# Feed-forward accumulators: the two column halves of a projection go to two PSUM banks instead of one

## The chip, the cores and the metric

The program runs on one core of a Trainium2 chip. Inside the core, TensorE (PE in the profile) multiplies matrices and writes the sums into PSUM, eight banks of 128 partitions by 512 fp32 columns; ScalarE (ACT) and VectorE (DVE) read PSUM and work in SBUF; the SyncE queue (SP) issues the transfers from memory. Engines run side by side and wait for one another by semaphores. The metric is the time of one execution in microseconds (us), lower being better.

## The reference, cut to what matters

The model is a two-layer encoder trunk over 256 tokens of width 1024, in float32. Each layer is a SwiGLU feed-forward, a token-mixing part and a second feed-forward, all added to the residual stream `h` after a gate; so there are four feed-forwards. The part that the change concerns:

```python
def swiglu(u, wg, wu, wd):
    return (jax.nn.silu(u @ wg) * (u @ wu)) @ wd
...
for l in range(DEPTH):                       # DEPTH = 2
    u = modulate(rmsnorm(h, norm_ffn1[l]), ...)
    h = h + 0.5 * (1.0 + mod[:, :, 2]) * swiglu(u, ffn1_wg[l], ffn1_wu[l], ffn1_wd[l])
    ...                                      # token mixing, ends in  mixed @ w_out[l]
    u = modulate(rmsnorm(h, norm_ffn2[l]), ...)
    h = h + 0.5 * (1.0 + mod[:, :, 8]) * swiglu(u, ffn2_wg[l], ffn2_wu[l], ffn2_wd[l])
```

`wg` and `wu` are 1024 x 2816, `wd` is 2816 x 1024.

## The kernel before

**Three matmuls for one.** Every fp32 weight and activation is split into a rounded high part and a remainder (`hi` and `lo` for weights, `uh` and `ul` for the normalised input `u`), and a product is the sum of hi x uh, hi x ul and lo x uh. `mm3` issues these three matmuls, each of 128 x 128 weights against 256 token columns, into the same 128 x 256 region of PSUM. This is the block of three that the title of the change speaks of.

**One feed-forward.** `ffn` runs over `j`, the 11 column groups of 256 of `wg` and `wu`. For one `j`, `proj` computes the gate projection: eight contraction chunks `k`, in each two column halves `f`, each a block of three, thus 48 matmuls. They go into one PSUM bank named `pg`: half `f = 0` in columns 0 to 255, half `f = 1` in columns 256 to 511. ACT applies silu to the whole bank (into `sg`); then 48 matmuls compute the up projection into another bank, `pu`; DVE multiplies `sg` by `pu`; `gated` splits the product into high and low parts (`g`). Then TensorE takes down projections (`out_unit`, tile `dn`) of earlier `j`, whose `g` has long been ready: 48 matmuls each, in 16 blocks of three, for eight row groups `d` of the output, two `d` to a bank in four banks. The four banks of `pg` and `pu` come from a ring (`bank`) of four, those of `dn` from the other four (`acc`). The j = 1 groups of the last three feed-forwards are done as a pair (`proj2`: gate and up interleaved). The first column groups of a feed-forward are done ahead of the loop (`start`: three in the first feed-forward, `lead`: one in the others, tiles `ld`). So in the first feed-forward the loop has eight `j`, in each of the others ten, one of them the pair: 38 in all, of which 35 are not pairs.

**The last down projection** goes through the row groups in pairs: twelve matmuls for `d` = 0 and 1, then DVE adds them to `h` (line 539), then the next pair. The output projection of token mixing (tile `wo`) uses the same function.

**The order of work** is written out by hand: each engine executes its instructions in the order in which the code names them. The weights come as a stream of 1 MB transfers (`raw_w`, and `raw_a` for the modulation weights) into four buffers. `half(n, hf)` asks for half of weight unit `n`; before it returns, `need` makes sure that the splits of all halves up to seven ahead (`AHEAD`) have been issued: `hi` on ACT (line 322) and `lo` on DVE (line 323). These splits therefore stand in ACT's queue among the silus: ahead of the silu of one `j` stand the splits of weights that are needed several units later, and each waits for its transfer. Eight `hi` and eight `lo` buffers hold the split halves, and the uses of TensorE free them.

Of the kernel before, what the change touches and what calls it, by code (L numbers as in the profile page):

```python
# [10 lines left out]
ALU = mybir.AluOpType  # L11
PSUM = bass.MemoryType.PSUM

P = 128
# [68 lines left out]
def downs(j, g0):  # L83
    done = 0
    for i in range(g0, j + 1):
        lo = done
        done = i if i - lo <= 2 else lo + 2
    return range(lo, done)
# [74 lines left out]
class Trunk:  # L163
# [352 lines left out]

    def out_unit(self, accs, n, mov, first, last, gate):
        nc = self.nc
        dst = lambda d: accs[d // 2][:, (d % 2) * 256:(d % 2) * 256 + 256]

        def block(w, d, f):
            st = first and f == 0 and d % 2 == 0
            self.mm3(dst(d), [w[0][:, d * P:(d + 1) * P], w[1][:, d * P:(d + 1) * P]], mov[f], st)

        if not last:
            for f in range(2):
                w = self.half(n, f)
                for d in range(8):
                    block(w, d, f)
                    if d % 2:  # L530
                        self.tick()
            return
        ws = [self.half(n, 0, 7), self.half(n, 1, 6)]
        for b in range(4):
            for d in (2 * b, 2 * b + 1):
                for f in range(2):
                    block(ws[f], d, f)
            for d in (2 * b, 2 * b + 1):
                nc.vector.scalar_tensor_tensor(out=self.h[:, d], in0=dst(d), scalar=gate[:, d:d + 1], in1=self.h[:, d],
                                               op0=ALU.mult, op1=ALU.add)  # L540
            if self.hg is None and b == 2:
                nc.scalar.preload_act_table_set(SET_SQRT)
            self.norm_a(b)
            if b == 2 or self.hg and b:
                self.norm_b(b - 1)
        if self.hg:
            self.norm_b(3)
# [10 lines left out]
    def proj_k(self, bank, w, k, flip, banks):  # L558
        w = [t[:, k % 4] for t in w]
        for f in range(2):  # L560
            if flip:
                self.mm3(banks[f], w, [t[:, f * P:(f + 1) * P] for t in self.u(k)], k == 0, True)
            else:
                cs = slice(f * P, (f + 1) * P)
                self.mm3(bank[:, f * 256:(f + 1) * 256], [t[:, cs] for t in w], self.u(k), k == 0 and f == 0)
# [17 lines left out]
    def ffn(self, w0, gate_col, prep, start=None):  # L583
        nc = self.nc
        self.open_acc(False)
        n = w0 + 2
        pend = []

        def gated(sg):
            g = self.tk4("g", FR)  # L590
            gh, gl = (g[:, 2 * i:2 * i + 2] for i in range(2))
            flat = lambda t: t.rearrange("p a b -> p (a b)")
            self.split(flat(gh), flat(gl), sg)
            pend.append([(gh[:, f], gl[:, f]) for f in range(2)])

        def ends(f, t, b):
            v = sg[:, (f % 2) * 256:(f % 2) * 256 + 256]
            if f < 2:
                self.silu(out=v, in_=t, bias=b)
            else:  # L600
                nc.vector.scalar_tensor_tensor(out=v, in0=t, scalar=b, in1=v, op0=ALU.add, op1=ALU.mult)

        g0 = 1
        if start:
            g0 = GS
            banks = start()
            n = w0 + 2 * GS
            self.need(n, 0, 2)
            for j in range(GS):
                sg = self.tk2("sg")  # L610
                self.silu(out=sg, in_=banks[2 * j])
                nc.vector.tensor_tensor(out=sg, in0=sg, in1=banks[2 * j + 1], op=ALU.mult)
                gated(sg)
        else:
            sg = self.tk2("sg")
            self.lead(w0, ends)
            gated(sg)
        accs = None
        for j in range(g0, NJ):
            pg, pu = self.bank("pg"), self.bank("pu")  # L620
            pair = j == 1
            if pair:
                self.proj2(n, (pg, False, None), (pu, False, None))
            else:
                self.proj(pg, n)
            sg = self.tk2("sg")
            self.silu(out=sg, in_=pg)
            if not pair:
                self.proj(pu, n + 1)
            nc.vector.tensor_tensor(out=sg, in0=sg, in1=pu, op=ALU.mult)  # L630
            gated(sg)
            if j == g0:
                accs = [self.acc("dn") for _ in range(4)]
            n += 2
            for i in downs(j, g0):
                self.out_unit(accs, n, pend.pop(0), i == 0, False, None)
                n += 1
            if start and j == 7:
                nc.sync.dma_start(out=self.consts, in_=self.io["consts"])
                nc.sync.dma_start(out=self.wdt, in_=self.io["wdt"])  # L640
        gate = self.gate(gate_col, True)
        prep()
        self.out_unit(accs, n, pend.pop(0), False, True, gate)
        self.close_acc()
# [469 lines left out]
```

## Time and profile before

| | us |
|---|---|
| median of 3 runs | 1152.15 (1152.0 to 1152.48) |
| the profiled execution: its time | 1152.72 |
| its span, first to last instruction | 1151.0 |
| PE busy | 1116.2 (97%) |
| DVE busy | 893.1 (78%) |
| ACT busy | 618.0 (54%) |
| hardware DMA queue, share of 16 engines | 64.6% |

The profile is of one execution on the one core. Busy time of PE is the union of the matmuls' records; a matmul's record is about 280 ns long and overlaps the next ones, so the pace is read from the distances of the starts, or from the chain that ended last, where 48 matmuls of one tile stand as one row with their time. The granted clock is the share of TensorE's full clock that was let through. A row of a timeline reads: start in us, duration in us, engine, line, operation, output tile <- input tiles, shape, count, and in brackets how long the engine had been idle before and what released it.

### The profile page before, as it was taken

To read this page: it belongs to the slowest core of one execution; us is meant where nothing else is said; L and a number is where in the kernel's file an instruction comes from. 1 tells how busy PE (TensorE), PEld (TensorE's weight loads), DVE (VectorE), ACT (ScalarE), POOL (GpSimd) and SP (SyncE) were. 2 spreads that over 40 slices of the span, in tenths; PEclk is the share of its full clock that TensorE was granted. 3 is DMA by queue.
4 is the path that set the end of the run, shared out by engine and by line. 5 is a ranking of instruction groups with operands and counts; after the bars stand their busy time and mean duration, and the time that the engine had idled before them with its cause. 6 is when DMAs were issued, how large, how long until landed. Compare 5 with 4: busy or idle time off the path is not lost.

```text
span 1151.0 us, 22045 instructions
## 1 busy us (share of the span) xinstructions
PE 1116.2 (97%) x9316; PEld 1105.1 (96%) x9316; DVE 893.1 (78%) x1300; ACT 618.0 (54%) x870; POOL 0.2 (0%) x4
## 2 busy tenths in 40 slices
PE   1999999999999999999999999999999999999996
PEld 1999999999999999999999999999999999999996
DVE  6988896788778789888588788667886877987544
ACT  4463444586874464444466444457687546544442
POOL 0000000000000000000000000000000000000000
PEclk9999999999999999999999999999999999999999
DMA  9879898357553449999636988653754452987610
GB/s 379 342 267 369 328 374 323 126 212 286 181 186 146 184 147 375 359 347 341 225 111 262 347 325 315 252 183 139 265 200 181 168 204 77 351 330 283 238 57 37
DMA packets 39556, 282.63 MB, mean 246 GB/s; under 512 B 4385, under 2 KB 4641, under 8 KB 5409
## 3 DMA queue, kind: packets, MB, share of 16 engines
q1 hardware_dynamic: 39456, 281.22, 64.6%
q8 instruction: 73, 1.20, 0.4%
q14 instruction: 27, 0.21, 0.1%
HBM read 280.15 MB, written 1.05 MB: 244 GB/s over the span
## 4 chain that ended last, share of the span: by engine, by line
PE 96%; DVE 2%; ACT 1%; DMA 1%; issue 0%; SPq 0%; ACTq 0%; DVEq 0%
PE dn L206 21%; PE pu L206 19%; PE pg L206 19%; PE pj L206 14%; PE ld L206 8%; PE wo L206 6%; PE pv L206 4%; DVE raw_a L282 1%; PE seg L206 1%; PE nps L206 1%; PE tail L206 1%; PE sz L206 1%; DMA h<-in_x 1%; PE rn L206 1%; PE yb L206 1%; PE rs L206 0%
## 5 line engine op out<-in xcount | busy, mean ns | idle before, releaser
L323 DVE TENSOR_TENSOR lo<-raw_w,hi 128x1024 fp32r<-128x1024 f32 x368 | 441.4, 1223 | 143.4 <-ACT hi L322 143.2
L322 ACT ACTIVATE hi<-raw_w 128x1024 fp32r<-128x1024 f32 x368 | 379.7, 1053 | 240.8 <-DMA raw_w<-in_w 107.5
L206 PE MATMUL dn<-g,hi 128*128 128x256 f32 x1408 | 250.4, 279 | 0.0
L206 PEld LDWEIGHTS dn<-g,hi 128*128 128x128 f32 x1408 | 215.1, 187 | 0.0
L282 DVE CUSTOM_DVE_ANT_0 raw_a<-raw_a,cond,params 128x1024 f32<-128x1024 f32 x160 | 198.9, 1280 | 0.5 <-DMA raw_a<-in_ada 0.5
L206 PE MATMUL dn<-g,lo 128*128 128x256 f32 x704 | 196.9, 280 | 0.0
L206 PE MATMUL pg<-uh,lo 128*128 128x256 f32 x608 | 170.1, 280 | 0.0
L206 PE MATMUL pu<-uh,lo 128*128 128x256 f32 x608 | 170.1, 280 | 0.0
L206 PE MATMUL pg<-uh,hi 128*128 128x256 f32 x608 | 169.8, 279 | 0.0
L206 PE MATMUL pu<-uh,hi 128*128 128x256 f32 x608 | 169.8, 279 | 0.0
L206 PE MATMUL pg<-ul,hi 128*128 128x256 f32 x608 | 169.6, 279 | 0.0
L206 PE MATMUL pu<-ul,hi 128*128 128x256 f32 x608 | 169.6, 279 | 0.0
L206 PEld LDWEIGHTS dn<-g,lo 128*128 128x128 f32 x704 | 132.2, 188 | 0.0
L206 PE MATMUL pj<-uh,hi 128*128 128x256 f32 x448 | 126.3, 282 | 0.0
L206 PE MATMUL pj<-ul,hi 128*128 128x256 f32 x448 | 124.4, 278 | 0.0
L206 PE MATMUL pj<-uh,lo 128*128 128x256 f32 x448 | 124.4, 278 | 0.0
L206 PEld LDWEIGHTS pg<-uh,lo 128*128 128x128 f32 x608 | 114.2, 188 | 0.0
L206 PEld LDWEIGHTS pu<-uh,lo 128*128 128x128 f32 x608 | 114.2, 188 | 0.0
L206 PEld LDWEIGHTS pu<-ul,hi 128*128 128x128 f32 x608 | 114.1, 188 | 0.0
L206 PEld LDWEIGHTS pg<-ul,hi 128*128 128x128 f32 x608 | 114.1, 188 | 0.0
L206 PEld LDWEIGHTS pg<-uh,hi 128*128 128x128 f32 x608 | 113.8, 187 | 0.0
L206 PEld LDWEIGHTS pu<-uh,hi 128*128 128x128 f32 x608 | 113.8, 187 | 0.0
(189 smaller groups left out, 1788.3 us busy)
## 6 DMA issues: line engine op xcount, KB each, us to landing
raw_w<-in_w SPq DMA_DIRECT2D x184, 1024.0 KB, 5.3
raw_a<-in_ada SPq DMA_DIRECT2D x80, 1024.0 KB, 6.4
consts<-in_consts SPq DMA_DIRECT2D x1, 1216.0 KB, 7.8
h<-in_x SPq DMA_DIRECT2D x1, 1024.0 KB, 6.6
out<-fin SPq DMA_DIRECT2D x4, 256.0 KB, 2.3
cond<-in_c SPq DMA_DIRECT2D x1, 512.0 KB, 4.3
mats<-in_mats SPq DMA_DIRECT2D x1, 256.0 KB, 6.8
params<-in_params SPq DMA_DIRECT2D x1, 176.0 KB, 4.6
```

The lines of the kernel that those rows point to most:

```text
L206: self.nc.tensor.matmul(out, lhsT=lhsT, rhs=rhs, start=start, stop=True, skip_group_check=True)
L282: nc.vector.tensor_tensor_reduce(out=raw[:, f * 1024:(f + 1) * 1024], in0=raw[:, f * 1024:(f + 1) * 1024], in1=self.cond, scale=1.0, scala ...
L322: self.nc.scalar.activation(out=hi, in_=src, func=AF.Copy)
L323: self.nc.vector.tensor_tensor(out=lo, in0=src, in1=hi.bitcast(F32), op=ALU.subtract)
```

## The change

Gate and up projection of one `j` now share two banks, both named `pgu`: in each bank, columns 0 to 255 are a half of the gate projection and columns 256 to 511 the same half of the up projection. Half `f` of either goes to bank `f`, so that consecutive blocks of three alternate between the two banks. The silu and the multiplication are each done as two instructions of 256 columns, one per bank, instead of one of 512. In `out_unit` row group `d` goes to bank `d % 4` instead of `d // 2`, so that there too consecutive row groups are in different banks. No matmul, no transfer and no byte of SBUF is added, removed or moved; the paddings that place the weights at 0 and the activations at 64 modulo 256 are as they were.

```diff
@@ out_unit
-        dst = lambda d: accs[d // 2][:, (d % 2) * 256:(d % 2) * 256 + 256]
+        dst = lambda d: accs[d % 4][:, (d // 4) * 256:(d // 4) * 256 + 256]
 
         def block(w, d, f):
-            st = first and f == 0 and d % 2 == 0
+            st = first and f == 0 and d < 4
             self.mm3(dst(d), [w[0][:, d * P:(d + 1) * P], w[1][:, d * P:(d + 1) * P]], mov[f], st)
@@ proj_k
+            elif flip is None:
+                cs = slice(f * P, (f + 1) * P)
+                self.mm3(bank[f], [t[:, cs] for t in w], self.u(k), k == 0 and banks)
             else:
                 cs = slice(f * P, (f + 1) * P)
                 self.mm3(bank[:, f * 256:(f + 1) * 256], [t[:, cs] for t in w], self.u(k), k == 0 and f == 0)
@@ ffn
         for j in range(g0, NJ):
-            pg, pu = self.bank("pg"), self.bank("pu")
+            two = [self.bank("pgu") for _ in range(2)]
+            pg, pu = ([t[:, o:o + 256] for t in two] for o in (0, 256))
             pair = j == 1
             if pair:
-                self.proj2(n, (pg, False, None), (pu, False, None))
+                self.proj2(n, (pg, None, True), (pu, None, False))
             else:
-                self.proj(pg, n)
+                self.proj(pg, n, None, True)
             sg = self.tk2("sg")
-            self.silu(out=sg, in_=pg)
+            for f in range(2):
+                self.silu(out=sg[:, f * 256:(f + 1) * 256], in_=pg[f])
             if not pair:
-                self.proj(pu, n + 1)
-            nc.vector.tensor_tensor(out=sg, in0=sg, in1=pu, op=ALU.mult)
+                self.proj(pu, n + 1, None, False)
+            for f in range(2):
+                v = sg[:, f * 256:(f + 1) * 256]
+                nc.vector.tensor_tensor(out=v, in0=v, in1=pu[f], op=ALU.mult)
             gated(sg)
```

Three places in the order of the instructions matter. The first is on PE, in the first feed-forward at `j = 4`, where the gate projection ends and the up projection begins. Names carry buffer numbers here (`hi10_1_706` is the high part of the second half of weight unit 10; `pg_895` and `pu_896` are one bank each). Before, the first matmul of `pu` waits for ACT's split of its weights, which is `hi11_0_735`:

```order
L206 MATMUL pg_895<-uh_92,lo10_1_706 128x256
L206 MATMUL pu_896<-uh_92,hi11_0_735 128x256 [waits Activation_49]
L206 MATMUL pu_896<-ul_93,hi11_0_735 128x256
L206 MATMUL pu_896<-uh_92,lo11_0_736 128x256 [waits DVE_49]
L206 MATMUL pu_896<-uh_92,hi11_0_735 128x256
```

The same place in the changed kernel:

```order
L206 MATMUL pgu_898<-uh_92,lo10_1_707 128x256
L206 MATMUL pgu_897<-uh_92,hi11_0_736 128x256 [waits Activation_49]
L206 MATMUL pgu_897<-ul_93,hi11_0_736 128x256
L206 MATMUL pgu_897<-uh_92,lo11_0_737 128x256 [waits DVE_49]
L206 MATMUL pgu_898<-uh_92,hi11_0_736 128x256 [waits Activation_49]
```

The count that the first matmul of the up projection waits for is now that of the silu of bank 897 (later in ACT's order than the split), and the first block into bank 898 has a wait of its own, for the silu of bank 898; before, `pu` was another bank than the one that the silu reads.

The second place is ACT's queue around that silu. Before:

```order
L322 ACTIVATE hi13_1_897<-raw_w13_502 128x1024 [waits PE_49,Activation_49]
L322 ACTIVATE hi14_0_931<-raw_w14_629 128x1024 [waits DMAHW5_49,PE_49,Activation_49]
L203 ACTIVATE sg_959<-pg_895 128x512 [waits PE_49]
L322 ACTIVATE hi14_1_961<-raw_w14_629 128x1024 [waits Activation_49]
L322 ACTIVATE hi15_0_995<-raw_w15_649 128x1024 [waits DMAHW7_49,PE_49,Activation_49]
```

In the changed kernel:

```order
L322 ACTIVATE hi13_1_899<-raw_w13_502 128x1024 [waits PE_49,Activation_49]
L322 ACTIVATE hi14_0_933<-raw_w14_629 128x1024 [waits DMAHW5_49,PE_49,Activation_49]
L203 ACTIVATE sg_961<-pgu_897 128x256 [waits PE_49]
L203 ACTIVATE sg_961<-pgu_898 128x256 [waits PE_49]
L322 ACTIVATE hi14_1_964<-raw_w14_629 128x1024 [waits Activation_49]
```

The silu stands where it stood, now in two, behind the split of weight unit 14, which waits for that unit's transfer (`DMAHW`).

The third place is on PE in the last down projection of the first feed-forward, where row group 4 begins. Before (bank 769 is the third of four, and nothing has read it yet):

```order
L206 MATMUL dn_768<-g_2228,hi32_1_2109 128x256 x2
L206 MATMUL dn_768<-g_2228,lo32_1_2110 128x256
L206 MATMUL dn_769<-g_2228,hi32_0_2079 128x256 x2
L206 MATMUL dn_769<-g_2228,lo32_0_2080 128x256
L206 MATMUL dn_769<-g_2228,hi32_1_2109 128x256 x2
```

In the changed kernel (here bank 769 is the first of four, which also holds row group 0):

```order
L206 MATMUL dn_772<-g_2244,hi32_1_2123 128x256 x2
L206 MATMUL dn_772<-g_2244,lo32_1_2124 128x256
L206 MATMUL dn_769<-g_2244,hi32_0_2093 128x256 [waits DVE_49]
L206 MATMUL dn_769<-g_2244,hi32_0_2093 128x256
L206 MATMUL dn_769<-g_2244,lo32_0_2094 128x256
```

Row group 4 now waits for DVE's update of `h` from row group 0, which reads the same bank; row groups 5, 6 and 7 wait likewise for those from 1, 2 and 3.

## The prediction

> **What bounds the kernel now.** I read the page first, then the chain that ended last, then the list of waits, then the timeline at the ends of the gate projections. The page's busy times and the chain's shares:
>
> ```profile
> PE 1116.2 (97%) x9316; PEld 1105.1 (96%) x9316; DVE 893.1 (78%) x1300; ACT 618.0 (54%) x870; POOL 0.2 (0%) x4
> PE 96%; DVE 2%; ACT 1%; DMA 1%; issue 0%; SPq 0%; ACTq 0%; DVEq 0%
> ```
>
> TensorE is the path, so the question is at what pace it goes and where it would begin to wait. Seven pieces of the chain in order of time (start, us, tile, matmuls):
>
> ```profile
> 143.46 5.65 PE pg L206 x48
> 149.11 5.65 PE pu L206 x48
> 154.76 5.65 PE dn L206 x48
> 241.57 29.93 PE pj L206 x264
> 276.95 4.24 PE pv L206 x36
> 282.90 6.88 PE pv L206 x60
> 329.87 7.11 PE pj L206 x60
> ```
>
> In the feed-forward every piece of 48 takes 5.65 us, 117.7 ns a matmul, and no piece waits for another. `pg` and `pu` stay in one bank for 48 matmuls and `dn` changes banks every six, at the same pace. In token mixing `pj`, in one bank and with the same two operand tensors as `pg`, runs 264 matmuls at 113.4 ns; `pv`, which alternates between two banks every three matmuls, runs 36 at 117.8 ns. So there are two paces, and neither bank layout owns one of them.
>
> **Alternating the banks by itself: nothing.** By `pv` at 117.8 ns against `pg` at 117.7 the alternation costs 0.1 ns or less. It concerns 38 x 96 + 44 x 48 = 5760 matmuls, so if it moved all of them to `pj`'s pace it would save 5760 x 4.4 ns = 25 us. I take 0 and keep 25 us for the range; the second stretch of `pv` (114.7 ns, with a break in it) says that alternating banks can be found at the faster pace too.
>
> **The new wait at the up projection.** Its first block now writes a bank that the silu must have read. These rows show the normal case, the last block of half 0, the last matmul of half 1, the first of `pu`, and the silu:
>
> ```profile
> 148.47 0.28 PE L206 MATMUL pg<-uh,lo 128*128 128x256 f32 x1
> 148.83 0.28 PE L206 MATMUL pg<-uh,lo 128*128 128x256 f32 x1
> 148.95 0.28 PE L206 MATMUL pu<-uh,hi 128*128 128x256 f32 x1
> 149.15 0.60 ACT L203 ACTIVATE sg<-pg 128x512 f32<-128x512 f32 x1 [0.86 <-PE pg L206]
> L457 ACT ACTIVATE rs<-nps 128x256 f32<-128x256 f32 x6 | 2.3, 386 | 6.9 <-PE nps L206 6.9
> L203 ACT ACTIVATE sg<-pg 128x512 f32<-128x512 f32 x38 | 22.5, 592 | 40.9 <-PE pg L206 40.9
> ACT sg L203 <- PE pg L206: 40.9, 24, 4.7
> ```
>
> ACT starts 0.04 us after the matmul that it waits for has ended (148.83 + 0.28 to 149.15). A silu of 256 PSUM columns is not in the trace; the ACT copy of 128x256 out of PSUM takes 0.39, and I take that. Half 0 ends at 148.75, its silu runs from 148.79 to 149.18, and with another 0.04 PE may go at 149.22 instead of 148.95: 0.27 us. A restart costs a little more, as the only long wait of PE on ACT shows, at half the clock (the second start comes 0.39 after the first, where 0.21 is the pace):
>
> ```profile
> 27.02 0.58 PE L206 MATMUL ld<-uh,hi 128*128 128x256 f32 x1 [10.35 <-ACT hi L322]
> 27.41 0.41 PE L206 MATMUL ld<-ul,hi 128*128 128x256 f32 x1
> 28.66 0.41 PE L206 MATMUL ld<-uh,hi 128*128 128x256 f32 x1
> 32.93 0.29 PE L206 MATMUL ld<-uh,lo 128*128 128x256 f32 x1
> ```
>
> That is 0.18 us, half of it at full clock: 0.36 us per wait. The second silu ends about 149.53, when the second block (149.22 + 0.09 + 0.35 = 149.66) has not yet come, so that wait is free. Low end 0.2 us (no latency), high end 0.5 (the second wait shows too).
>
> Behind the waiting matmul stands all of TensorE's work, so the whole wait lengthens the path. Of the 38 silus three belong to pairs, which have no such wait; 35 remain. In 24 of these ACT stood ready and waited for PE, as the last row shows; in the other 11 ACT came late, which before cost nothing, because nothing but the multiplication after `pu` needed the silu.
>
> **Where ACT is late.** The first matmul of `pu`, and the silu, in the first, second and last feed-forward:
>
> ```profile
> 69.80 0.28 PE L206 MATMUL pu<-uh,hi 128*128 128x256 f32 x1
> 71.37 0.58 ACT L203 ACTIVATE sg<-pg 128x512 f32<-128x512 f32 x1
> 430.68 0.28 PE L206 MATMUL pu<-uh,hi 128*128 128x256 f32 x1
> 438.29 1.06 ACT L322 ACTIVATE hi<-raw_w 128x1024 fp32r<-128x1024 f32 x1 [2.87 <-DMA raw_w<-in_w]
> 439.26 0.58 ACT L203 ACTIVATE sg<-pg 128x512 f32<-128x512 f32 x1
> 447.64 0.28 PE L206 MATMUL pu<-uh,hi 128*128 128x256 f32 x1
> 452.70 0.58 ACT L203 ACTIVATE sg<-pg 128x512 f32<-128x512 f32 x1
> 985.84 0.28 PE L206 MATMUL pu<-uh,hi 128*128 128x256 f32 x1
> 991.98 0.58 ACT L203 ACTIVATE sg<-pg 128x512 f32<-128x512 f32 x1
> 427.00:443.00 16.00, 16.00 (x138) 16.00 (x137) 15.33 (x20) 6.50 (x7) 0.00 (x0) 1.00 0.99 386
> ```
>
> At 430.68 the silu stands behind a split whose transfer lands only at 438.29. TensorE now waits for it: 439.26 + 0.39 + 0.04 + 0.09 - 430.68 = 9.1 us. Likewise 6.7 us at 985.84 and 2.1 us at 69.80 (there behind splits, not a transfer): 17.9 us together. The later late silus are covered: once PE stands 9.1 us later, the next silu (452.70 against 447.64, 5.1 late) is ready before PE comes, provided the transfers do not stand still while PE does. They don't have to: the last row (a window, clock, DMA share and GB/s at its end) has the transfers at 0.99 of the time and 386 GB/s there, so they are behind on their own account. The remaining 32 waits cost the normal 0.36: 11.5 us (6.4 to 16).
>
> **The clock after the two long waits.** The end of the trace shows when the grant falls (windows; the last three columns are the clock, the DMA share and GB/s):
>
> ```profile
> 1138.89 2.83 PE L206 MATMUL mean<-sq,mats 128*128 128x256 f32 x12 [0.25 <-DVE sq L444]
> 1143.00:1145.00 2.00, 0.00 (x0) 0.00 (x0) 1.97 (x3) 0.23 (x1) 0.00 (x0) 1.00 0.00 0
> 1145.00:1146.00 1.00, 0.00 (x0) 0.00 (x0) 1.00 (x3) 1.00 (x4) 0.00 (x0) 0.83 0.00 0
> PE nps L206 <- DVE diag L360: 2.5, 6, 1.7
> ```
>
> PE ends at 1141.72 and the mean 0.83 puts the fall to half at 1145.66, 3.9 us later. Waits of 9.1 and 6.7 us exceed that, 2.1 us doesn't, and the longest wait for `diag`, 1.7 us, was no cause either. After a fall TensorE goes at half pace until it has worked for a while: at the start from about 28.28 to 32.93, 20 matmuls in 4.27 us from 28.66 on, 213.5 ns each. 4.65 us at that pace lose 4.65 x (1 - 117.7 / 213.5) = 2.1 us; twice, 4.2 us. Low end 0 (no fall), high end 5. The Trainium skill ("TensorE: Matmul & The Clock Gate", Part 1: The HAM clock gate) has the clock halve after an idle window of about 3.4 us and return after a busy one as long; the trace's 3.9 us agrees within its free-running window, and 3.4 us instead of 4.65 would make this term an estimated 3.0 instead of 4.2.
>
> **The last down projections.** Row group 4 now shares a bank with group 0, so it waits for DVE to have read that:
>
> ```profile
> 213.61 0.87 DVE L539 SCALAR_TENSOR_TENSOR h<-dn,gate,h 128x256 f32<-128x256 f32 x2
> 213.96 0.40 PE L206 MATMUL dn<-g,hi 128*128 128x256 f32 x2
> ```
>
> The first of the two DVE instructions takes 0.48 of the 0.87 and ends at 214.09; with latency and restart PE goes 0.26 late. There are six such ends (four feed-forwards, two output projections); if all were like this it would be 1.6 us, if DVE came a little earlier in each, 0. I take 1.0. The other groups' waits come 0.3 us and more after their reads.
>
> **The doubled small operations.** ACT gets 38 x (2 x 0.39 - 0.59) = 7 us, DVE about as much in 38 halved multiplications. They cost nothing: the products are used one down projection or more later (5.65 us). If that cover were gone, each `j` would pay some 0.2 us, 7 us in all.
>
> **Sum.** 17.9 + 11.5 + 4.2 + 1.0 = 34.6 us on the profiled execution's own 1152.7 us (span 1151.0) gives 1187.3. That execution is 0.6 us above the median, so I say 1187. With each term at its ends it runs from 1176 to 1198.
>
> **The rivals.**
> - *The faster pace.* Each new wait starts TensorE's pipeline afresh, and it might settle at 113.4 ns. Against it: the piece of `pj` at 329.87 follows other work and keeps 118.5 ns, its break included. If all 5760 matmuls did, 1187 - 25 = 1162; if half, 1175. Still slower.
> - *The lateness is not absorbed.* If the transfers stood still while PE waits, the second feed-forward's silus would be late again and again, each by some 5 us as at 447.64; six more of these and 3 us in the last feed-forward give 1187 + 33 = 1220. The 0.99 speaks against it.
> - *The other side: not slower.* If consecutive blocks into one bank cost PE its excess over the pure stream, alternation frees it. Half-clock matmuls at 213.5 ns, twice 106.8, give the floor: 11 ns x 5760 = 63 us saved, 1124. It decides from 34.6 us / 5760 = 6.0 ns on, a pace of 111.7 ns. Against it: no stretch in the trace is that fast, and `pv` alternates at 117.8.
> - *A clock that falls at every short wait.* The 35 waits at 2.1 us each in place of two: 1187 + 69 = 1256. That 1.7 us waits did not do it speaks against it. The Trainium skill ("TensorE: Matmul & The Clock Gate", A second HAM failure mode: psum-queue depth-cycling) warns that cycling through banks lets the clock oscillate; here `dn` cycles through four banks without it.
>
> **Chances.** My sum 71%, the faster pace in part or whole 13%, lateness not absorbed 6%, the falling clock 2%, the other side 8%, of which 3% stop within 0.2% (2.3 us, about what a measurement of this kernel can tell from no change). So faster 0.05, same 0.03, slower 0.92. The range, 1166 to 1200, takes in the sum's ends and most partial forms of the faster pace; the likeliest case's own is 1176 to 1198.
>
> **What the next profile would show.** Right: `pgu` waiting for ACT's silu in the list of PE's waits, 35 times, two of them 6 to 9 us long, near 436 and 1009 us; a clock below 1 behind these two; 5.65 us pieces otherwise. Wrong: pieces of 48 at 5.4 us (faster pace), several long waits in one feed-forward (not absorbed), or no wait of PE on ACT at all.

## The result and the profile after

The changed kernel takes 1189.41 us (median of 4 runs, 1188.81 to 1191.47) against 1152.32 (4 runs, 1152.0 to 1152.8): 1.0325 times as long, interval 1.0307 to 1.0343. Predicted were 1187 us and a range of 1166 to 1200. The profiled execution took 1188.81 us, its span 1187.0, which is 36.0 more than before.

The busy times and the shares of the chain, from the page of the changed kernel:

```profile
PE 1129.2 (95%) x9316; PEld 1110.5 (94%) x9316; DVE 897.7 (76%) x1338; ACT 626.1 (53%) x908; POOL 0.2 (0%) x4
PE 85%; DVE 6%; ACT 4%; DMA 3%; issue 1%; SPq 0%; ACTq 0%; DVEq 0%
L203 ACT ACTIVATE sg<-pgu 128x256 f32<-128x256 f32 x76 | 27.2, 382 | 43.1 <-PE pgu L206 43.0
```

TensorE has the same 9316 matmuls, but its share of the chain falls from 96% to 85%: 13% of the span now hangs on DVE, ACT and transfers, where it was 4%. The silu of 256 columns takes 0.382 us on average (0.39 was taken). The list of PE's waits (in total, times, longest, in us) has a row that before had not:

```profile
PE nps L206 <- DVE sq L444: 11.9, 1, 11.9
PE ld L206 <- ACT hi L322: 10.3, 1, 10.3
PE pgu L206 <- ACT sg L203: 19.5, 5, 9.7
PE nps L206 <- DVE diag L360: 2.5, 6, 1.7
```

It counts five waits for the silu, not 35. The other thirty are too short for this list, because the record of the matmul before still runs when they begin; they are read from the distances between starts. The normal case, in the timeline of PE and of ACT at 134 us:

```profile
133.59 0.28 PE L206 MATMUL pgu<-ul,hi 128*128 128x256 f32 x1
133.71 0.28 PE L206 MATMUL pgu<-uh,lo 128*128 128x256 f32 x1
134.11 0.39 PE L206 MATMUL pgu<-uh,hi 128*128 128x256 f32 x1
134.33 0.28 PE L206 MATMUL pgu<-ul,hi 128*128 128x256 f32 x1
133.67 0.73 ACT L203 ACTIVATE sg<-pgu 128x256 f32<-128x256 f32 x2 [1.48 <-PE pgu L206]
```

From 133.71 to 134.11 are 0.40 us where 0.12 is the pace, then 0.22: a wait of 0.28 and a restart of 0.10. One `j` of the second feed-forward, in the chain (start, us, tile, matmuls), runs from 470.55 to 487.91, 17.36 us, where three pieces of 5.65 made 16.95:

```profile
470.55 5.65 PE dn L206 x48
476.21 5.31 PE pgu L206 x45
481.98 5.93 PE pgu L206 x48
487.91 5.65 PE dn L206 x48
```

The longest wait, at 446 us, in the timelines of PE and ACT, and the two stretches of low clock as windows (the last three columns are clock, DMA share and GB/s):

```profile
436.04 0.28 PE L206 MATMUL pgu<-uh,lo 128*128 128x256 f32 x1
445.97 0.58 PE L206 MATMUL pgu<-uh,hi 128*128 128x256 f32 x1 [9.65 <-ACT sg L203]
446.35 0.41 PE L206 MATMUL pgu<-ul,hi 128*128 128x256 f32 x1
444.59 1.06 ACT L322 ACTIVATE hi<-raw_w 128x1024 fp32r<-128x1024 f32 x1 [4.64 <-DMA raw_w<-in_w]
445.55 0.64 ACT L203 ACTIVATE sg<-pgu 128x256 f32<-128x256 f32 x2
438.70:448.90 10.20, 2.93 (x13) 2.93 (x14) 8.63 (x11) 3.80 (x6) 0.00 (x0) 0.50 0.98 384
1012.20:1022.30 10.10, 5.76 (x27) 5.76 (x28) 8.26 (x10) 5.00 (x7) 0.00 (x0) 0.50 0.99 368
```

The silus stand behind a split that begins when its transfer has landed, at 444.59; the first of the two ends 0.04 us before PE goes. The DMA engines are busy at 0.98 throughout: they did not stand idle, the transfer was late.

Added up over the feed-forwards and output projections, as the distance of each matmul's start from the one before, less 117.8 ns: four long waits 20.0 us, 31 short ones with their restarts 12.3, 39 matmuls at the half clock 4.1, last down projections and output projections 1.0, less 0.85 for one stretch of 193 matmuls at 113.4 ns, and 0.2 of rest: 36.7, against the 36.0 by which the span grew.

### The profile page after: what moved, and what is told of

Same layout as the page of the kernel before. It is cut to its first block, busy times and chain, and to the rows that moved or that the text cites. A ratio compares the mean times of both kernels' runs of the same rounds, so it can differ in the third digit from the quotient of the medians.

```text
span 1187.0 us, 22112 instructions
## 1 busy us (share of the span) xinstructions
PE 1129.2 (95%) x9316; PEld 1110.5 (94%) x9316; DVE 897.7 (76%) x1338; ACT 626.1 (53%) x908; POOL 0.2 (0%) x4
## 4 chain that ended last, share of the span: by engine, by line
PE 85%; DVE 6%; ACT 4%; DMA 3%; issue 1%; SPq 0%; ACTq 0%; DVEq 0%
PE pgu L206 31%; PE dn L206 19%; PE pj L206 13%; PE ld L206 7%; PE wo L206 6%; PE pv L206 4%; DMA raw_w<-in_w 2%; DVE lo L323 2%; ACT hi L322 1%; DVE raw_a L282 1%; ACT sg L203 1%; DVE nt L462 1%; PE seg L206 1%; DVE ul L468 1%; PE nps L206 1%
## 5 line engine op out<-in xcount | busy, mean ns | idle before, releaser
L206 PE MATMUL pgu<-uh,hi 128*128 128x256 f32 x1216 | 345.1, 284 | 23.2 <-ACT sg L203 19.5
L206 PE MATMUL pgu<-uh,lo 128*128 128x256 f32 x1216 | 341.8, 281 | 0.0
L206 PE MATMUL pgu<-ul,hi 128*128 128x256 f32 x1216 | 341.2, 281 | 0.0
L206 PEld LDWEIGHTS pgu<-uh,hi 128*128 128x128 f32 x1216 | 229.5, 189 | 30.3 <-ACT sg L203 30.3
L206 PEld LDWEIGHTS pgu<-ul,hi 128*128 128x128 f32 x1216 | 230.5, 190 | 0.0
L206 PEld LDWEIGHTS pgu<-uh,lo 128*128 128x128 f32 x1216 | 230.0, 189 | 0.0
L206 PEld LDWEIGHTS pj<-uh,hi 128*128 128x128 f32 x448 | 84.1, 188 | 0.7 <-issue 0.7
L206 PEld LDWEIGHTS pj<-ul,hi 128*128 128x128 f32 x448 | 84.2, 188 | 0.0
L206 PEld LDWEIGHTS pj<-uh,lo 128*128 128x128 f32 x448 | 84.0, 188 | 0.0
L323 DVE TENSOR_TENSOR g<-sg,g 128x512 fp32r<-128x512 f32 x44 | 30.5, 693 | 30.7 <-ACT g L322 30.7
```

Source lines behind the costliest of these rows:

```text
L206: self.nc.tensor.matmul(out, lhsT=lhsT, rhs=rhs, start=start, stop=True, skip_group_check=True)
L323: self.nc.vector.tensor_tensor(out=lo, in0=src, in1=hi.bitcast(F32), op=ALU.subtract)
```

## The experiments

What is to be told apart: (1) the alternation itself costs nothing and the sharing of banks makes TensorE wait (the prediction's theory); (2) alternating banks changes TensorE's own pace, down or up; (3) within the first, whether the long waits come from where the silu stands in ScalarE's order, or from transfers that would be late anyway.

**Alternation without sharing.** Each half of the gate and of the up projection gets a bank of its own, so that blocks alternate as in the changed kernel, but no bank holds both; `out_unit` is that of before.

```diff
-            two = [self.bank("pgu") for _ in range(2)]
-            pg, pu = ([t[:, o:o + 256] for t in two] for o in (0, 256))
+            pg, pu = ([self.bank(x)[:, 0:256] for _ in range(2)] for x in ("pg", "pu"))
```

> The change with one thing taken out: gate and up projection no longer share a bank. The gate projection's halves alternate between two banks of their own and the up projection's between two others (all four ring banks per column group), the silu and the product still in two halves; the down projection's banks as in the kernel before. The alternation of banks is therefore whole, the new waits are not. Theory (all of the loss is waiting, none is alternation): no wait of PE on ACT in the feed-forward, pieces of 48 matmuls at 5.65 us, 1152 to 1154 us. Rival (writing alternate banks costs or saves something per matmul): a pace other than 117.8 ns in pieces of the gate and up projection; at 113.4 ns 1136 us, and if alternation carried even a third of the loss 1164 us or more.

Measured: 1151.27 us, 0.9996 times before (0.9973 to 1.0019). The runs lie in two groups, six from 1153.98 to 1155.25 and five from 1147.74 to 1148.56, with one at 1144.87; what sets them apart comes below. The profiled execution is one of the upper group. Its chain, and the only new row among PE's waits:

```profile
125.26 5.65 PE pg L206 x48
130.91 5.65 PE pu L206 x48
136.56 5.65 PE dn L206 x48
PE pu L206 <- DVE lt L502: 1.5, 3, 0.5
```

The pieces take 5.65 us as before, with every block in another bank than the one ahead of it. The three waits are those of the pairs, whose banks DVE has yet to read; with their restarts they cost 2.3 us, about the distance of the upper group from before (1152.68, median of 25 runs on that chip). Alternation by itself costs nothing and brings nothing.

**The down projections alone.** Before, with `d % 4` and `d // 4` in `out_unit`.

```diff
-        dst = lambda d: accs[d // 2][:, (d % 2) * 256:(d % 2) * 256 + 256]
+        dst = lambda d: accs[d % 4][:, (d // 4) * 256:(d // 4) * 256 + 256]
-            st = first and f == 0 and d % 2 == 0
+            st = first and f == 0 and d < 4
```

> The kernel before with only the down projection's part of the change: row group d in bank d % 4, so that row group 4 of a last down projection waits for the update of row group 0. Theory: five of the six ends wait 0.13 to 0.29 us, sum 1.0 us, everything else unchanged: 1153.0 to 1153.7 us. Rival (this wait was hidden and the change there is free): 1152.0 to 1152.6 us. Second rival (row groups in alternating banks change the pace of 2112 matmuls): a pace of dn other than 117.8 ns, 1143 us at 113.4.

Measured: 1153.39 us, 1.0012 times before (0.9992 to 1.0032). In the trace the ends of the feed-forwards cost 0.8 us and those of the output projections 0.25. That is as expected, but the timing does not tell it from no change.

**The silu two places earlier.** After, with fewer splits asked for by the gate projection.

```diff
-                self.proj(pg, n, None, True)
+                self.proj(pg, n, None, True, 4)    # half() asks for 4 splits ahead, was 7
```

> The changed kernel, but with the gate projection asking for weight splits only four halves ahead instead of seven, so that the silu stands in ACT's queue before three splits that it stood behind; the up projection then asks for seven again. Theory (the long waits are the silu standing behind splits that wait for their transfers): the four long waits shrink to the short 0.39 us, the clock does not fall, and 1189.4 - 1.6 - 1.1 - 9.5 - 6.4 - 4.1 = 1166.7 us, 1165 to 1169. Rival (the transfers themselves are the limit once TensorE depends on them, and the wait only moves to the weights): a wait of PE on a split of about the same length, 1180 us or more. In both, the 35 short waits stay.

Measured: 1177.06 us, 1.0224 times before (1.0192 to 1.0257): of the fall expected, about half. The chain and the waits in the second feed-forward:

```profile
429.95 6.35 DMA raw_w<-in_w
437.79 7.27 PE pgu L206 x48
445.05 5.65 PE dn L206 x48
PE pgu L206 <- ACT sg L203: 8.7, 3, 4.4
```

The wait at 446 us shrank from 9.8 to 4.3 us, the one at 1016 from 6.8 to 4.6, the two others became short ones. What I had missed: the down projection ahead still asks for 7, so the silu had moved past two splits, not three. How much the two places gave depends on when the splits stood there. In the changed kernel ScalarE's rows are these (the split at 444.59, the last ahead of the silu at 446 us, is shown above):

```profile
437.95 2.00 ACT L322 ACTIVATE hi<-raw_w 128x1024 fp32r<-128x1024 f32 x2 [5.08 <-DMA raw_w<-in_w]
1012.74 2.00 ACT L322 ACTIVATE hi<-raw_w 128x1024 fp32r<-128x1024 f32 x2 [6.31 <-DMA raw_w<-in_w]
1015.16 1.06 ACT L322 ACTIVATE hi<-raw_w 128x1024 fp32r<-128x1024 f32 x1 [0.42 <-DMA raw_w<-in_w]
```

The silu now stands behind the first split of the row of two (437.95, 1012.74) instead of behind the split that follows that row (444.59, 1015.16). These two lie 6.6 us apart at 446 us, and the wait became 5.5 us shorter; they lie 2.4 us apart at 1016 us, and it became 2.2 us shorter. So the length of the wait goes by the time of the last split ahead of the silu, and with it by that split's transfer. The short waits, 33 of 0.39 us, stayed, and the clock fell again.

**And the order of the blocks at the seam.** As the last, and the last two chunks of the gate projection and the first two of the up projection are done half by half instead of alternating, so that the silu of a half has six matmuls of time before its bank is written.

```diff
+            if flip is None and k in (0, 1, 6, 7):
+                if k % 2 == 0:
+                    for f in range(2):
+                        for kk in (k, k + 1):
+                            ...
```

> As the kernel with four halves ahead, and in addition the last two chunks of the gate projection and the first two of the up projection go half by half (two chunks of half 0, then two of half 1), so that the silu of half 0 has six matmuls of time instead of three. Banks stay shared and the halves stay in different banks. Theory (a short wait is silu latency, 0.28 us, plus 0.11 for the restart): six matmuls are 0.71 us against the 0.63 that matmul end, silu and two signals take, so all short waits go, 35 x 0.39 = 13.6 us: 1153.0 to 1155 us, of which 1 us is the ends of the last down projections. Rival (the restart or the bank, not the silu, makes the short wait): the waits stay, 1165 us or more.

Measured: 1162.54 us (1157.25 to 1169.56), 1.0101 times before (1.0066 to 1.0136). In the profiled execution (span 1158.7) no short wait of 0.28 us is left. Two long ones (9.0 us), the half clock behind them (5.3), the last down projections (0.9) and 1.6 us in steps of 0.04 to 0.07 at the seams are, and 1864 matmuls went at 113.4 ns, 8.3 us less: 8.5 in all, against 7.7 by which the span stands above before. The time is 9 us over the expected one because the two long waits stayed, as they did in the last kernel. That the 33 short waits went with the order at the seam was right.

The small steps are the silu's as well. At one seam, the silu of half 0 and the weight loads (PEld) of the last matmul ahead of the seam and of the first behind it:

```profile
454.74 0.39 ACT L203 ACTIVATE sg<-pgu 128x256 f32<-128x256 f32 x1 [3.21 <-PE pgu L206]
455.02 0.19 PEld L206 LDWEIGHTS pgu<-uh,lo 128*128 128x128 f32 x1
455.18 0.19 PEld L206 LDWEIGHTS pgu<-uh,hi 128*128 128x128 f32 x1
```

The second load begins 0.16 us after the first, where 0.12 is the pace, and 0.05 us after the silu's end at 455.13: the load of the waiting matmul waits too. In the trace of before such a load runs one matmul ahead (148.83, for the matmul at 148.95); in the changed kernel it begins together with its matmul, at 134.11. That fits the restart of 0.10 us behind each short wait.

**The silu ahead of every late split.** After, with 4, 4, 4 and 3 positions asked for by the down projection's and the gate's halves; the seam is that of the changed kernel.

```diff
-                w = self.half(n, f)                                  # out_unit, not the last
+                w = self.half(n, f, None if gate is not None else 4)
-                self.proj(pg, n, None, True)
+                self.proj(pg, n, None, True, (4, 3))
```

> After, with fewer weight splits asked for ahead of a gate's silu: the halves of the down projection and of pg are asked for 4, 4, 4 and 3 positions ahead in place of 7, so that on ScalarE no split later than two halves after the first that pu uses stands before the silu; the splits left out follow right behind it. The sharing of banks, and so the 31 short waits, stay. The theory (the long waits are lateness of a transfer that stands ahead of the silu in ScalarE's order): the long waits (20.0 us in after's trace) and the half clock behind them (4.1) go, the short ones (12.3) stay: 1165 to 1166 us, and up to 8 less if a stretch falls into the pace of 113.4 ns. The rival (the transfers themselves are late, and splits done later put them off further): matmuls wait for hi in place of the silu, 1170 or more.

Measured: 1169.63 us (1167.31 to 1174.7), 1.0167 times before (1.0142 to 1.0191). The profiled execution, the fastest, has a span of 1165.5, a clock of 0.998 as before, and this row:

```profile
PE pgu L206 <- ACT sg L203: 2.9, 8, 0.7
```

The long waits went from 19.5 us in the list to nothing over 0.7, and no clock fell: it is the silu's place behind late splits that made them. By the distances between starts the 35 waits cost 15.5 us, 0.44 each, and the last down projections 1.7, less 0.7 for 162 matmuls at 113.4 ns: 16.5, while the span grew by 14.5; 1.3 us of the difference lie ahead of the first gate projection, which began earlier in this execution (62.99 us instead of 64.31). The 1165 to 1166 that I expected had the waits at 0.39. The other runs, of which there is no trace, are 1.5 to 7.4 us above this one, more than the theory says; two of the three lie above the 1170 of the rival, which is therefore not excluded for them.

**Both mended.** The last kernel with the seam of the one before it.

> The kernel of e5_ahead, and the first two and last two chunks of pg and pu done bank by bank instead of alternating, so that each half's silu starts six matmuls ahead of the next writer of its bank. Alternation stays for the middle four chunks, the sharing of banks for all. The theory: short and long waits gone, what is left over before is the last down projections (0.6) and wo (0.25): 1153.4 us, less by up to 8 if stretches fall into the faster pace as in e4_both. A rival by which alternation itself, or the sharing itself, costs something beyond the waits: 1157 or more.

Measured: 1166.04 us (1162.54 to 1168.33), 1.0118 times before (1.0097 to 1.0139). The expected 1153.4 was missed by 12.6 us, and what came is above the rival's bound of 1157; its reason must be read from the trace. The distances add up to 15.3 us: five waits for a silu of 1 to 2.4 us and three of 0.35 (8.9 us together), 2.9 of half clock behind two of them, 1.1 of restarts, 2.8 at the last down projections, 1.1 in the small steps at the other seams, less 1.5 for two fast stretches. One of the long ones, in the chain, and the same place in ScalarE's timeline (L644 is the multiplication of the `j` before):

```profile
122.14 7.79 DMA raw_w<-in_w
131.13 1.23 DVE lo L323
134.01 7.32 PE pgu L206 x48
130.04 1.06 ACT L322 ACTIVATE hi<-raw_w 128x1024 fp32r<-128x1024 f32 x1 [4.53 <-DMA raw_w<-in_w]
133.05 0.63 ACT L322 ACTIVATE g<-sg 128x512 fp32r<-128x512 f32 x1 [1.95 <-DVE sg L644]
133.59 0.64 ACT L203 ACTIVATE sg<-pgu 128x256 f32<-128x256 f32 x2
```

A transfer lands at 130.0; its split on ACT, then the low part on DVE (to 132.4), the multiplication of the `j` before behind that, the copy `g` behind the multiplication, and the silu behind the copy: a longer way from the late transfer to the silu, through two queues. In the kernel with the same seam, but four positions asked for by the gate alone, the split of this unit began earlier, since its transfer was issued at 117.62 instead of 122.14:

```profile
117.62 0.33 SPq L268 DMA_DIRECT2D raw_w<-in_w  x1
125.20 1.06 ACT L322 ACTIVATE hi<-raw_w 128x1024 fp32r<-128x1024 f32 x1 [5.13 <-DMA raw_w<-in_w]
```

125.20 against 130.04, with PE at about the same place. Each of the two issues comes 0.02 us after DVE has ended the low part of an earlier unit (117.60 and 122.12). Splits that are done later free their buffers later, and the transfers into these start later: so the traces read, and the rival of the last kernel ("the transfers themselves are late") has its share here. The last kernel, without the mended seam, has the same chain at the same place:

```profile
122.04 0.33 SPq L268 DMA_DIRECT2D raw_w<-in_w  x1
128.82 1.06 ACT L322 ACTIVATE hi<-raw_w 128x1024 fp32r<-128x1024 f32 x1 [4.10 <-DMA raw_w<-in_w]
```

Its transfer landed 1.2 us earlier, and the wait was 0.9 us instead of 2.4. So the late asking makes a wait at this place without the new seam too; why the transfer took 1.1 us longer with it stays open, and no run tries it by itself. The 15.3 us lie in waits, half clock and restarts, not in the pace: by these traces sharing two banks has no price beyond the waits that it makes.

**Two paces.** In every trace TensorE goes at 117.8 ns or at 113.4, for hundreds of matmuls on end. To see whether an odd matmul turns the one into the other, four variants of before got matmuls whose result is overwritten. First one or six of 264 columns ahead of the second group of each feed-forward:

```diff
+            if j == g0:
+                w = self.half(n, 0, 1)
+                self.w[n, 0] = w
+                for _ in range(1):                 # or 6
+                    self.mm(pu[:, 0:264], w[0][:, 0, 0:P], ..., True)
```

> Before, with one matmul of 264 columns into the bank of pu, whose result is overwritten, ahead of the second group of each feed-forward part. It tests what sets the pace of 117.8 or 113.4 ns. If the pace is a phase of the matmul stream that a break or an odd-sized matmul can set (in before, pj runs at 113.4 after pv's matmuls of 264 columns): stretches of the feed-forward at 113.4, 4.4 ns less per matmul, down to 1127 us if all of them. If banks, operands or tile sizes set it: 117.8 as before, 1152.5 us.

> As j264 with six such matmuls in each place. Phase: a second chance of another draw, between 1127 and 1153; and if one draws the fast pace and the other not, the number of odd columns matters. Banks, operands or sizes: 1153.2 us (six matmuls of about 0.12 in each feed-forward part).

Measured: 1152.9 us with one (0.9997, 0.9981 to 1.0013) and 1151.63 with six (0.9992, 0.9967 to 1.0018); no change in the median. But the ten runs with six lie in steps: five from 1154.12 to 1156.09, four from 1148.05 to 1149.13, one at 1142.33. The profiled execution is one of the middle group, and its chain says what a step is; in the second feed-forward and in the last:

```profile
431.45 5.65 PE pu L206 x48
437.10 5.65 PE dn L206 x48
1046.86 5.44 PE pg L206 x48
1052.30 5.44 PE pu L206 x48
1057.74 5.44 PE dn L206 x48
```

From 965 us to its end the last feed-forward goes at 113.4 ns, some 1480 matmuls; 4.4 ns each are 6.5 us, the distance between the groups. In the same program, with the same banks, the other three go at 117.8. The groups of the kernel without sharing stand as far apart; of its faster groups there is no trace.

Then one such matmul ahead of every `pg` and `pu`, of 264 or of 320 columns, and last four groups of six in each feed-forward, between groups of six of 256 columns, as `pv` and `pj` stand in token mixing:

```diff
+            if k == 0 and odd:
+                self.mm(bank[:, 0:264], w[0][:, 0, 0:P], ..., True)       # or 320
```

> Before, with one matmul of 264 columns (its result is overwritten) ahead of every pg and pu of the feed-forward parts that is done by itself: some 70 of them. It asks what turns the pace of 117.8 ns into that of 113.4. In the mixer of every trace so far, groups of six matmuls of 264 columns stand between groups of six of 256, and the 256s run at 113.4 after each fourth group and at 117.8 after the others. If the pace hangs on the sum of columns modulo 64 (six times 8 columns, four times, is 192), each such matmul moves it by 8 and every eighth stretch runs at 113.4: 1152.5 + 70 x 0.121 - 1/8 of 25 us = 1158 us, with fast stretches eight places apart. If an odd matmul only gives a new draw: fast stretches at no regular distance.

> As ev264 with 320 columns. Columns modulo 64: such a matmul moves nothing, every stretch stays at 117.8 (but where a feed-forward part starts at 113.4, all of it): 1152.5 + 70 x 0.14 = 1162 us. A new draw by any odd matmul: fast stretches here too.

> Before, with the mixer's pattern in each of the four feed-forward parts: in the second pg that is done by itself, four groups of six matmuls of 264 columns (their result is overwritten), one behind the six matmuls of each of the first four chunks. In the mixer of all traces the 256-column matmuls run at 113.4 ns after the fourth such group. If the pattern sets the pace wherever it stands: each feed-forward part runs at 113.4 from there on, 1152.1 + 96 x 0.121 - some 4 x 1350 x 4.4 ns = 1140 us, faster than both kernels. If it is a draw, as the six of j264x6 were (their runs stood near 1155.5, 1148.5 and 1142.3, none, one or two parts at the faster pace): 1164 less 6 for each part that draws it, 1152 to 1164 with a scatter from run to run.

Measured: 1160.49, 1163.17 (one run each) and 1164.15 us (1.0105, 1.0088 to 1.0122). No feed-forward stretch of these three traces is at 113.4 ns for more than six matmuls. The sum of columns modulo 64 is wrong, and so is the pattern as a switch; a single odd matmul moves the pace in none of some 140 places. None of the kernels beats before beyond its interval.

## Why the prediction was right

- *Alternation by itself, 0.* Right: 5.65 us a piece, with the sharing taken away. The rival of the other side (not slower, a pace of 111.7 ns or less) has nothing left: no stretch of the feed-forwards was faster than 113.4.
- *Short waits, 32 of 0.36, 11.5 us.* Measured 31 of 0.39, 12.1 to 12.3: 0.28 for the silu (0.27 said) and 0.11 for the restart (0.09 said). That the second half's wait is free was right. The list of waits was the wrong place to look for 35 of them: it shows five.
- *Long waits, 17.9 us.* Measured 20.0. The one at 1016 us was 6.8 (6.7 said), the one at 71.6 was 2.1 (2.1 said). Two parts of the difference: at 446 us it was 9.8 instead of 9.1, and at 169.88 stood a fourth, 1.45 us, that I had as a short one. Its transfer, too, landed late, as this piece of the chain says:

```profile
161.08 7.32 DMA raw_w<-in_w
169.88 5.92 PE pgu L206 x48
```

  The step that failed is that I read each lateness off the trace of before as if the transfers kept their times. Before, the two transfers were issued at 431.78 and 159.31 (the split of the second is the third row); in the changed kernel the first was issued at 437.31:

```profile
431.78 0.33 SPq L268 DMA_DIRECT2D raw_w<-in_w  x1
159.31 0.33 SPq L268 DMA_DIRECT2D raw_w<-in_w  x1
164.67 1.06 ACT L322 ACTIVATE hi<-raw_w 128x1024 fp32r<-128x1024 f32 x1 [3.21 <-DMA raw_w<-in_w]
437.31 0.33 SPq L268 DMA_DIRECT2D raw_w<-in_w  x1
```

  At 446 us the issue moved by 5.5 us, as far as TensorE had, but from issue to split went 7.3 us instead of 6.5 (438.29 before, 444.59 now). At 169.88 the issue moved by 1.8 us and TensorE by 2.6, and from issue to split (168.50) went 7.4 us instead of 5.4. So the transfers follow the shifted work and then take longer, by 0.8 and 2.1 us; why they take longer, no run shows.
- *Lateness is absorbed afterwards.* Right: behind 446 us each `j` is 0.4 us longer and no more.
- *The clock falls twice, 4.2 us.* Measured 4.1: 39 matmuls at the half clock, about the 20 each that the start had shown. It came 2.4 us after the end of the last matmul at 436.32, earlier than the 3.9 at the end of the trace of before. The stretches at 0.50 last 10.24 us each in the trace's clock records, and 3.41, 6.83 in those of the experiments: multiples of 3.41. This agrees with the Trainium skill ("TensorE: Matmul & The Clock Gate", Part 1: The HAM clock gate), which has a free-running window of 3.413 us; the estimate of 3.0 us by that page's figure, which stood beside mine, lies further from the 4.1. The step from 3.9 us to "2.1 us doesn't" did not hold: in the kernel with both mended the clock also fell behind waits of 2.37 and 2.05 us (the windows from 133.80 to 137.10 and from 734.60 to 737.80 are at 0.50), the second time 1.4 us after TensorE had gone on at 733.03. Behind the wait of 1.98 us that ended at 71.59 in the changed kernel it stayed at 1.00. That this one brought no third fall was in part luck.
- *The clock falling at every short wait.* It didn't: two stretches of low clock inside the feed-forwards, both behind waits of over 6 us, and none in the kernel that alternates without sharing. What the Trainium skill ("TensorE: Matmul & The Clock Gate", A second HAM failure mode: psum-queue depth-cycling) warns of is not seen here.
- *Last down projections, 1.0.* Measured 1.0: 0.29, 0.19, 0.29 and twice 0.13.
- *Doubled small operations, 0.* ACT's busy time grew by 8.1 us, DVE's by 4.6, and no wait of a down projection for them shows.
- *The faster pace.* It came once, 193 matmuls behind the wait at 71.59, 0.85 us. In other kernels it took whole feed-forwards, but the waits do not bring it on as a rule.

The sum was 34.6 against 36.0, right term by term to within 2.1 us, with the misses in the long waits. The upper end that the prediction gives its sum, 1198, does not come out of its terms: with each at its high end they make 1193, and 1200 with the 7 us of the doubled operations. The measured 1189 lies under all three.

## What to carry to other kernels

Before two stages share a PSUM bank, ask who reads it between them, and where that reader stands in its own queue: the reader's 0.38 us cost 0.4 per seam, but the queue ahead of it, splits that wait for transfers, cost 1.5 to 10 us at a time and the half clock on top. Work that nothing waited for (a late silu) becomes the path the moment that its input's bank is to be written again. A reader can be moved ahead in its queue, but what it is moved past may free buffers for the transfers; that is a price of its own.

## What the runs showed that I had not expected

TensorE has two lasting paces for the same stream of 256-column matmuls, 117.8 and 113.4 ns, at the full clock; a stretch keeps its pace over hundreds of matmuls and changes it only at a break or behind groups of odd-sized ones. A whole feed-forward in the faster one is 6.5 us. In the one run of a middle group that was traced it is what sets runs of one kernel apart in steps (1155, 1148.5, 1142); for the other steps their distance speaks. In token mixing the faster pace followed the same group of `pv` in all thirteen traces; in the feed-forward it came and went from run to run. What sets it stays open: banks, operands and the sum of columns modulo 64 are excluded by these runs, and a way to bring it on was not found. A kernel that held it in all 5760 matmuls of the feed-forwards' loops and output projections would save an estimated 25 us (4.4 ns each).
